# Strassen's seven block products for the feed-forward of a hybrid encoder block

## The chip, the core and the metric

One core of a Trainium2 chip runs the whole block as one program. TensorE (PE) multiplies matrices, VectorE (DVE), ScalarE (ACT) and GpSimd (POOL) do the element-wise work, SyncE (SP) issues the transfers between DRAM and the on-chip memory (SBUF) on one queue, which 16 DMA engines work off. Matrix products are accumulated in PSUM, eight banks of 128 x 512 float32. The metric is the device time in microseconds (us), as the median of several executions. One execution is profiled; its rows stand below.

## The reference, cut to what matters

For one sequence of 2048 tokens with 1024 features, all in float32:

```python
mod = silu(c) @ w_ada + b_ada                      # shift, scale, gate for two sub-layers
x = x + gate1 * (mixer(rms_norm(x) ...) @ w_out)   # recurrent and attention heads
h2 = rms_norm(x, norm2_g) * (1.0 + scale2) + shift2
ff = jnp.square(jax.nn.relu(h2 @ w_ff1)) @ w_ff2   # 1024 -> 4096 -> 1024
x = x + gate2 * ff
return rms_norm(x, final_g)
```

The change touches the last four lines.

## The kernel before, in words

A product of two float32 matrices is made from three products of rounded halves: each operand is split into a high part (a copy in the rounded type `F32R`) and a low part (the operand less its high part, rounded in turn), and PE adds high x high, high x low and low x high in one PSUM bank. So a block of 128 x 128 x 512 costs three matmuls of 512 columns. Every matmul is issued by the helper `mm` (line 87); the splits of weights are made by `wsplit` (line 240): the high part by ACT (line 91), the low part in two pieces of 512 columns by POOL (line 250) or in one by DVE (line 252).

The program is traced in Python. Its tiles are named by a tag (`sbt`), each tag has a fixed number of buffers (`BUFS`), and a planner sets the order of the instructions on each engine from the order in which they are traced, from its own costs and from when buffers come free. An engine, and SP's queue as well, then works off its instructions in that fixed order; one that waits holds those behind it. `later`, `tick`, `side` and `step` spread small pieces of work between larger ones while the program is traced.

In the mixer's output stage `out_a` makes one tile of 128 tokens after another (24 matmuls each; tiles 8 to 15 first, then 0 to 7). `norm2` normalises it. Tiles 8 to 15 are stored in DRAM (`Dx1`); tiles 0 to 7 stay in SBUF, in the four accumulators `acc_`. `build` transposes four tiles at a time by PE (line 315, four transposes to a bank) and splits the result (lines 332 to 334) into `h2T`.

The feed-forward runs over two halves of 1024 tokens, first tiles 0 to 7, then 8 to 15. In each half it goes through the 32 groups of 128 hidden columns. `ff1` multiplies a group's weights, from DRAM, with the half's tokens, in two groups of 512 tokens with 24 matmuls each, then squares the positive part (ACT lines 1257 and 1258, DVE line 1259, POOL line 1260 for the low part). `ff2_tile` multiplies the group's hidden block with the second layer's weights, which `ff_w2` has scaled by the gate (line 245): per tile of tokens two banks of 3 matmuls (6 for the first and last two groups), each added by DVE to its accumulator (line 1276), which starts as the residual. So nothing of the hidden layer leaves SBUF. The second layer of one group runs between pieces of the first layer of the next. When a half is through, `final` normalises each tile (POOL line 294, DVE lines 292 to 299 and 1291) and stores it (line 1292).

Of the kernel before, what the change touches and what calls it, by code (L numbers as in the profile page):

```python
# [56 lines left out]
def block_kernel(ctx: ExitStack, tc, x, vecs, pos, w_ada, b_ada, fg, w_in, lwa, lwx, w_out, w1, w2, cst, out):  # L57
# [3 lines left out]
    sb = ctx.enter_context(tc.tile_pool(name="sb", bufs=1))  # L61
# [7 lines left out]
    def sbt(tag, shape, dt=F32):  # L69
        cnt[0] += 1  # L70
        return sb.tile(list(shape), dt, tag=tag, name=f"{tag}_{cnt[0]}", bufs=BUFS[tag])
# [62 lines left out]
    Dx1 = [drt(f"Dx1{t}", (P, D)) for t in range(NT // 2)]  # L134
# [1026 lines left out]
    acc_ = [sbt("L8", (P, 2, D)) for _ in range(4)]  # L1161
    r2s = cpt("r2s", (P, 8))
    order = list(range(8, 16)) + list(range(8))
    la_ = {}

    def load_a(t):
        if t < 8:
            xt = acc_[t // 2][:, t % 2]
        else:
            if t % 2 == 0:  # L1170
                la_["pair"] = sbt("L8", (P, 2, D))
            xt = la_["pair"][:, t % 2]
# [4 lines left out]
    h2T = [None, None]  # L1177
    xn = {}

    def norm2(t, xt):  # L1180
# [3 lines left out]
        if t >= 8:  # L1184
            later(lambda: SY.dma_start(Dx1[t - 8], xt), 1)
        for r2 in rstd_g(ss, D, r2s[:, t - 8:t - 7] if t >= 8 else None):
            yield
        if t < 8:
            if t % 2 == 0:
                xn["pair"] = sbt("L8", (P, 2, D))  # L1190
            xn[t] = xn["pair"][:, t % 2]
            V.tensor_scalar(xn[t], xt, r2[:, 0:1], None, ALU.mult)
# [14 lines left out]
    bld = iter(())  # L1207
    for i, t in enumerate(order):
# [7 lines left out]
        out_a(t)  # L1216
        step(2)
        run(bld, 4)
        if i + 3 < NT:
            load_a(order[i + 3])  # L1220
        if t == 5:
            h2T[0] = new_hT()
            bld = build([xn[e] for e in range(4)], h2T[0], gs2, sh2)
    flush()
    run(bld)
    built = [last[:], None]
    h2T[1] = new_hT()
    bld = build([xn[e] for e in range(4, 8)], h2T[1], gs2, sh2)


    gate2 = sbt("bc", (P, D))
    SY.dma_start(gate2, Dbc[1])
    fgb = sbt("bc", (P, D))
    bcast_row(fgb, fg, D)

    def ff_w1(i):
        w = wsplit(wraw(w1[i]), A, G)
        return w.rearrange("p s (k c) -> p s k c", k=8)

    def ff_w2(i):  # L1240
        e = V if i < FV else G
        return wsplit(wraw(w2[i * P:(i + 1) * P, :]), A, e, row=gate2, row_eng=e)

    def ff1(w, hid, g):
        pt = pst("tr")
        n = 0
        hT = h2T[g]
        for k in range(8):
            hi, lo = hT[k // 4][:, k % 4, :], hT[2 + k // 4][:, k % 4, :]
            for l, r in ((w[:, 0, k, :], hi), (w[:, 0, k, :], lo), (w[:, 1, k, :], hi)):  # L1250
                mm(pt, l, r, n == 0, n == 23)
                n += 1
            if k % 4 == 3:
                if k == 7:
                    cs = slice(512 * g, 512 * (g + 1))
                    r_ = sbt("t2", (P, 512))
                    A.activation(r_, pt, AF.Relu)  # L1257
                    A.activation(hid[:, 0, cs], r_, AF.Square)
                    V.tensor_tensor(r_, r_, r_, ALU.mult)  # L1259
                    G.tensor_tensor(hid[:, 1, cs], r_, f(hid[:, 0, cs]), ALU.subtract)  # L1260
                yield

    nb = [0]

    def ff2_tile(t, parts):
        ts = slice(t * P, (t + 1) * P)
        for hf in range(2):
            cs = slice(512 * hf, 512 * (hf + 1))
            pt = pst("mm" if nb[0] % 2 else "g")
            nb[0] += 1  # L1270
            for i, (w, hid) in enumerate(parts):
# [6 lines left out]
    def ff2(parts):  # L1278
        for t in range(8):
            ff2_tile(t, parts)  # L1280
            if t % 2 == 1:
                yield
# [130 lines left out]
```

## Time and profile before

| | us |
|---|---|
| median of 3 runs | 2800.24 |
| lowest and highest | 2793.2, 2805.78 |
| the profiled execution | 2808.67 |
| its span, first to last instruction | 2806.9 |
| PE busy in it | 2685.0 |

In a page of the profile the busy time of an engine is its share of the span; the strips cut the span into 40 slices of 70 us and give tenths. A line such as L87 is that of the helper that issued the instruction, so groups are told apart by their tiles: `ptr<-hT,wh` are the first layer's matmuls, `pg<-wh,L` and `pmm<-wh,L` the second's. The mean of one matmul is longer than its place in the sequence, since they are pipelined; the place is had from a count over a stretch. In the rows of stretches come start and end, the length, for each engine the busy us and the number of instructions, then the granted clock (1.00 is 2.4 GHz), the share of the 16 DMA engines' time and GB/s.

### The profile page before, as it was taken

How to read it: one execution, taken by the hardware profiler on the slowest of the kernel's cores; microseconds unless marked ns; L12 is line 12 of the kernel's file. 1: busy time of each engine (PE TensorE's matmuls, PEld its weight loads, DVE VectorE, ACT ScalarE, POOL GpSimd, SP SyncE). 2: the span in 40 equal slices, each digit the busy share in tenths (PEclk: the TensorE clock that was granted, in tenths of full speed). 3: DMA queues.
4: the chain of work that ended last, by engine and by line, in shares of the span. 5: the costliest groups of instructions: out<-in, count | busy, mean ns of one | idle time of the engine just before them, and what ended most of it. 6: DMA issues, size and time to landing. Idle time of an engine off the chain costs nothing.

```text
span 2806.9 us, 33193 instructions
## 1 busy us (share of the span) xinstructions
PE 2685.0 (96%) x12089; PEld 2209.7 (79%) x12089; DVE 1645.0 (59%) x3174; ACT 801.2 (29%) x1173; POOL 1093.1 (39%) x833
## 2 busy tenths in 40 slices
PE   4988998999999999999899999999999999999998
PEld 3766777778888888878688888888878888888886
DVE  6688787965434444546645555555575555555555
ACT  2244675561222222223321112121142211211112
POOL 2443444632211221322444444444445444454442
PEclk9998999998899889899999999999999999999999
DMA  6765347566445545467111111111133111111111
GB/s 258 270 213 184 96 165 253 174 161 165 111 114 136 120 118 125 120 190 240 68 53 46 46 45 46 53 53 46 46 119 144 53 46 46 46 53 53 46 38 60
DMA packets 178783, 309.83 MB, mean 110 GB/s; under 512 B 79018, under 2 KB 112550, under 8 KB 171050
## 3 DMA queue, kind: packets, MB, share of 16 engines
q1 hardware_dynamic: 178620, 307.72, 35.2%
q8 instruction: 95, 1.56, 0.2%
q14 instruction: 68, 0.56, 0.1%
HBM read 230.83 MB, written 76.64 MB: 110 GB/s over the span
## 4 chain that ended last, share of the span: by engine, by line
PE 48%; DVE 2%; POOL 0%; issue 0%; ACT 0%; DMA 0%; POOLq 0%; DVEq 0%; ACTq 0%
PE ptr L87 24%; PE pg L87 12%; PE pmm L87 12%; DVE L L1276 0%; DVE L L1291 0%; POOL ry L294 0%; POOL hT L334 0%; DVE r L1300 0%; DMA r<-Dx 0%; POOL wh L250 0%; PE ptr L315 0%; DVE hT L334 0%; DVE hT L333 0%; ACT st L332 0%; DVE ry L299 0%
## 5 line engine op out<-in xcount | busy, mean ns | idle before, releaser
L250 POOL TENSOR_TENSOR wh<-r,wh 128x512 fp32r<-128x512 f32 x332 | 477.9, 1462 | 716.5 <-ACT wh L91 539.0
L87 PE MATMUL ptr<-hT,wh 128*128 128x512 f32 x3072 | 744.5, 392 | 4.0 <-POOL hT L334 2.1
L87 PEld LDWEIGHTS ptr<-hT,wh 128*128 128x128 f32 x3072 | 579.1, 189 | 129.2 <-ACT st L332 3.2
L1276 DVE TENSOR_TENSOR L<-pg,L 128x512 f32<-128x512 f32 x480 | 331.3, 690 | 565.3 <-PE pg L87 564.5
L87 PE MATMUL pg<-wh,L 128*128 128x512 f32 x1536 | 434.4, 394 | 0.0
L87 PE MATMUL pmm<-wh,L 128*128 128x512 f32 x1536 | 434.3, 394 | 0.0
L87 PE MATMUL pmm<-hT,wh 128*128 128x512 f32 x1536 | 377.6, 402 | 6.4 <-POOL hT L334 3.6
L1257 ACT ACTIVATE t<-ptr 128x512 f32<-128x512 f32 x128 | 76.8, 600 | 1003.4 <-PE ptr L87 1003.4
L87 PEld LDWEIGHTS pmm<-hT,wh 128*128 128x128 f32 x1536 | 294.8, 194 | 79.6 <-POOL hT L334 8.1
L87 PEld LDWEIGHTS pmm<-wh,L 128*128 128x128 f32 x1536 | 288.1, 188 | 68.8
L87 PEld LDWEIGHTS pg<-wh,L 128*128 128x128 f32 x1536 | 288.2, 188 | 66.6 <-POOL L L1260 0.4
L1276 DVE TENSOR_TENSOR L<-pmm,L 128x512 f32<-128x512 f32 x480 | 330.0, 688 | 10.5 <-PE pmm L87 8.6
L846 DVE CUSTOM_DVE_ANT_0 junk<-ptr,mb 128x256 bf16<-128x256 f32 (+2 forms) x384 | 140.1, 365 | 173.8 <-PE ptr L87 156.3
L1260 POOL TENSOR_TENSOR L<-t,L 128x512 fp32r<-128x512 f32 x128 | 166.9, 1305 | 179.0 <-DVE t L1259 179.0
L900 ACT ACTIVATE t<-pmm 128x512 f32<-128x512 f32 x160 | 95.1, 596 | 357.0 <-PE pmm L87 355.8
L294 POOL TENSOR_TENSOR ry<-rv,mhalf 128x1 f32<-128x1 f32 x80 | 52.3, 655 | 329.5 <-DVE rv L292 324.2
L87 PE MATMUL pmm<-hT,hT 66*128 66x256 f32 (+5 forms) x672 | 175.7, 396 | 0.0
L87 PE MATMUL ptr<-hT,hT 128*128 128x256 f32 (+5 forms) x672 | 163.2, 390 | 4.1 <-DVE mc L846 4.0
L87 PE MATMUL pg<-t,L 128*66 128x192 f32 (+2 forms) x756 | 156.6, 344 | 2.7 <-POOL L L1039 2.7
L91 ACT ACTIVATE wh<-r 128x1024 fp32r<-128x1024 f32 x128 | 135.1, 1057 | 80.7 <-PE pmm L87 69.2
L87 PEld LDWEIGHTS pmm<-hT,hT 128*128 128x128 f32 (+1 forms) x672 | 147.6, 276 | 8.4 <-issue 2.3
L87 PEld LDWEIGHTS ptr<-hT,hT 128*128 128x128 f32 (+1 forms) x672 | 142.0, 278 | 13.7 <-DVE mc L846 7.0
(211 smaller groups left out, 2990.3 us busy)
## 6 DMA issues: line engine op xcount, KB each, us to landing
r<-in_w SPq DMA_DIRECT2D x128, 512.0 KB
L<-in_w_ada SPq DMA_DIRECT2D x24, 1024.0 KB
r<-in_w_in SPq DMA_DIRECT2D x40, 512.0 KB
r<-in_x SPq DMA_DIRECT2D x26, 512.0 KB
hT<-Dq SPq DMA_DIRECT2D x21, 512.0 KB
hT<-Dk SPq DMA_DIRECT2D x21, 512.0 KB
Dh<-hT SPq DMA_DIRECT2D x8, 1024.0 KB
Dq<-st SPq DMA_DIRECT2D x32, 256.0 KB
```

The costliest lines, as they stand in the source:

```text
L87: T.matmul(o, l, r, start=st, stop=sp, skip_group_check=True)
L91: A.activation(o, i, AF.Copy)
L250: G.tensor_tensor(w[:, 1, cs], raw[:, cs], f(w[:, 0, cs]), ALU.subtract)
L294: G.tensor_tensor(y, v_, mhalf[:, 0:1], ALU.pow)
L846: V.tensor_tensor_reduce(junk[:, 0:nk], p_[:, e, 0:nk], mb1[:, off:off + nk], 1.0, -3e38, ALU.add, ALU.max, mc[:, idx:idx + 1])
L900: A.activation(pf, pS, AF.Exp)
L1257: A.activation(r_, pt, AF.Relu)
L1260: G.tensor_tensor(hid[:, 1, cs], r_, f(hid[:, 0, cs]), ALU.subtract)
L1276: V.tensor_tensor(o, pt, o, ALU.add)
```

## The change

Both layers are cut into 2 x 2 blocks and multiplied by Strassen's seven products. With A the weights or hidden blocks on the left and B the right operand, the tables `LEFT` and `RIGHT` name the one or two blocks that are added (or subtracted) for each product: (11, 1, 22) is block 11 plus block 22, (21, 0, 0) block 21 alone.

The mixer's output stage now keeps all 16 tiles' residual in DRAM (`Dx1`) and stores the normed and transposed tokens there too (`Dh2`, float32, unsplit). Then the buffers of the stages before are given up and laid out anew (`f1`). The first layer goes over two halves of 1024 tokens, in each over seven products, in each over 16 steps `p` of 128 hidden rows: a step adds its weight blocks, splits the sum, and issues 12 matmuls. The product's right operand is made once per product by `b_prep`, while the product before runs. `evac1` adds the bank to the blocks of the hidden layer that need it. Hidden blocks 12 and 21 are ready after products 3 and 4; they go to DRAM (`Dhh`) and are loaded again in products 6 and 7, where the seven left operands of the second layer are formed and stored (`Dhx`).

The second layer lays the buffers out once more (`f2`). It goes over seven products, each over 16 steps with 24 matmuls: eight tiles of tokens, each in its own PSUM bank, accumulate over the 16 steps. A step loads a hidden operand (512 KB) and one or two weight blocks. `evac2` adds the banks to the output tiles `C`. In the last product `finals` multiplies `C` by the gate, adds the residual and normalises; that product's own weights carry the gate.

```diff
-    Dx1 = [drt(f"Dx1{t}", (P, D)) for t in range(NT // 2)]
+    Dx1 = [drt(f"Dx1{t}", (P, D)) for t in range(NT)]
+    Dh2 = [{(k, j): drt(f"Dh2{a}{k}{j}", (P, 4, 512)) for k in (1, 2) for j in (1, 2)} for a in range(2)]
+    Dhh = [{i: drt(f"Dhh{a}{i}", (16, P, 512)) for i in (12, 21)} for a in range(2)]
+    Dhx = {m: drt(f"Dhx{m}", (16, P, 2, 512)) for m in range(1, 8)}
...
+    def build2(a, j, ts):
+        for k in range(8):
+            p_ = tr_bank(ts, k)
+            t = sbt("st", (P, 512))
+            A.activation(t, p_, AF.Identity, scale=gs2[:, k:k + 1], bias=sh2[:, k:k + 1])
+            yield
+            SY.dma_start(Dh2[a][k // 4 + 1, j][:, k % 4], t)
...
+        if i % 4 == 1 and i > 4:
+            t0 = order[i - 5]
+            bld.append(build2((i - 5) // 8, (i - 5) // 4 % 2 + 1, [xn[e] for e in range(t0, t0 + 4)]))
...
+    LEFT = {1: (11, 1, 22), 2: (21, 1, 22), 3: (11, 0, 0), 4: (22, 0, 0), 5: (11, 1, 12), 6: (21, -1, 11), 7: (12, -1, 22)}
+    RIGHT = {1: (11, 1, 22), 2: (11, 0, 0), 3: (12, -1, 22), 4: (21, -1, 11), 5: (22, 0, 0), 6: (11, 1, 12), 7: (21, 1, 22)}
+    stage.close()
+    NP = DFF // P // 2
+    BUFS.update({"c21": NP, "c11": NP, "c22": NP, "wr": 4, "wf": 3, "hx": 7})
...
+    def halves(raw, hi, lo, lo_eng):
+        A.activation(hi, raw, AF.Copy)
+        lo_eng.tensor_tensor(lo, raw, f(hi), ALU.subtract)
+    ORD1 = (2, 4, 5, 3, 1, 6, 7)
...
+    def w1_prep(s):
+        _, m, p = steps1[s]
+        x_, y_ = raws1.pop(s)
+        if LEFT[m][1]:
+            t = sbt("st", (P, 512))
+            signed(V, t, x_, LEFT[m][1], y_)
+        else:
+            t = x_
+        w = sbt("wf", (P, 2, 512), F32R)
+        halves(t, w[:, 0], w[:, 1], V if m == 7 else G)
...
+    def b_prep(a, m):
+        hi, lo = sbt("L8", (P, 4, 512), F32R), sbt("L8", (P, 4, 512), F32R)
...
+        for k in range(4):
+            t = sbt("st", (P, 512))
+            SY.dma_start(t, Dh2[a][x_ // 10, x_ % 10][:, k])
+            if sg:
+                t2 = sbt("st", (P, 512))
+                SY.dma_start(t2, Dh2[a][y_ // 10, y_ % 10][:, k])
+            yield
+            if sg:
+                signed(V, t, t, sg, t2)
+            halves(t, hi[:, k], lo[:, k], V)
+            yield
...
+    def evac1(s, pt):
...
+        elif m == 3:
+            h = c.pop((12, p))
+            V.tensor_tensor(h, pt, h, ALU.add)
+            V.tensor_tensor(c[22, p], pt, c[22, p], ALU.add)
+            yield
+            sq_relu_v(h)
+            yield
+            SY.dma_start(Dhh[a][12][p], h)
...
+        elif m == 6:
+            h = c[22, p]
+            V.tensor_tensor(h, pt, h, ALU.add)
+            sq_relu_a(h)
+            yield
+            x2, x7 = hx.pop((s, 12)), hx.pop((s, 21))
+            V.tensor_tensor(x2, x2, h, ALU.add)
+            V.tensor_tensor(x7, x7, h, ALU.subtract)
+            yield
+            put(a, 4, p, h)
+            put(a, 2, p, x2)
+            put(a, 7, p, x7)
+        else:
+            h, h22 = c.pop((11, p)), c.pop((22, p))
+            V.tensor_tensor(h, pt, h, ALU.add)
+            sq_relu_a(h)
+            yield
+            x1_, x5, x6 = sbt("st", (P, 512)), hx.pop((s, 21)), hx.pop((s, 12))
+            V.tensor_tensor(x5, x5, h, ALU.add)
+            G.tensor_tensor(x1_, h, h22, ALU.add)
+            G.tensor_tensor(x6, x6, h, ALU.subtract)
+            yield
+            put(a, 3, p, h)
+            put(a, 5, p, x5)
+            put(a, 1, p, x1_)
+            put(a, 6, p, x6)
...
+    LW, LP = 4, 2
...
+    for s, (a, m, p) in enumerate(steps1):
...
+        if s + LW < N1:
+            w1_load(s + LW)
+        if s + 2 < N1:
+            hx_load(s + 2)
+        if s + LP < N1:
+            w1_prep(s + LP)
...
+        for k in range(4):
+            ks = slice(k * P, (k + 1) * P)
+            for l, r in ((w[:, 0, ks], hi[:, k]), (w[:, 0, ks], lo[:, k]), (w[:, 1, ks], hi[:, k])):
+                mm(pt, l, r, n == 0, n == 11)
+                n += 1
...
+    BUFS.update({"C": NT, "xr": 4, "w2": 4, "wf": 4, "xt": 2, "row": 2})
+    ORD2 = (4, 2, 7, 3, 5, 1, 6)
...
+    def prep2(s):
...
+            signed(V, t, x_, RIGHT[m][1], y_)
+            if m == 6:
+                V.tensor_tensor(t, t, gate2[:, 512:], ALU.mult)
...
+        halves(t, w[:, 0], w[:, 1], V)
...
+        A.activation(h[:, 0], r_, AF.Copy)
+        for e in range(2):
+            G.tensor_tensor(h[:, 1, e], r_[:, e], f(h[:, 0, e]), ALU.subtract)
...
+    def resid(t, eng):
+        xt = sbt("xt", (P, D))
+        SY.dma_start(xt, Dx1[t])
+        yield
         for hf in range(2):
             cs = slice(512 * hf, 512 * (hf + 1))
+            eng.tensor_tensor(C[t][:, cs], C[t][:, cs], gate2[:, cs], ALU.mult)
+        yield
+        for hf in range(2):
+            cs = slice(512 * hf, 512 * (hf + 1))
+            eng.tensor_tensor(C[t][:, cs], C[t][:, cs], xt[:, cs], ALU.add)
...
+    for s, (m, p) in enumerate(steps2):
+        if s + L2 < N2:
+            ld2(s + L2)
+        if s + P2 < N2:
+            prep2(s + P2)
+        w, h = wts2.pop(s), hids.pop(s)
+        if p == 0:
+            pts = [pst(("mm", "g", "tr")[i % 3]) for i in range(8)]
+        for i in range(8):
+            ts = slice(i * P, (i + 1) * P)
+            mm(pts[i], h[:, 0, ts], w[:, 0], p == 0, False)
+            mm(pts[i], h[:, 0, ts], w[:, 1], False, False)
+            mm(pts[i], h[:, 1, ts], w[:, 0], False, p == NP - 1)
+            if p == NP - 1:
+                evac2(m, i, pts[i])
+                if m == 6:
+                    step(2)
+        if m == ORD2[-1]:
+            if p == 0:
+                fin = finals()
+            if p >= 1:
+                run(fin, 6)
```

Where the loads and stores of a step go: `w1_load` loads one or two blocks of 128 x 512 from `w1` (two of one row block in one transfer), `hx_load` the two blocks of `Dhh` in products 6 and 7, `put` stores a block in `Dhx`, `ld2` loads a hidden operand of `Dhx` and one or two blocks of `w2`.

## Rows read from the trace of the kernel before

**Rows 1.** The page: busy time of the engines; the granted clock in 40 slices.

```profile
PE 2685.0 (96%) x12089; PEld 2209.7 (79%) x12089; DVE 1645.0 (59%) x3174; ACT 801.2 (29%) x1173; POOL 1093.1 (39%) x833
PEclk9998999998899889899999999999999999999999
```

**Rows 2.** Busy time by stretch, the feed-forward in full run.

```profile
core 0: us, PE busy (x) PEld busy (x) DVE busy (x) ACT busy (x) POOL busy (x), PEclk, DMA share, GB/s
1500.00:1700.00 200.00, 200.00 (x869) 162.95 (x869) 108.34 (x162) 39.24 (x54) 93.80 (x63) 1.00 0.14 48
```

**Rows 3.** Groups by line, 1352-2807 us: count | busy us, mean ns | idle.

```profile
L87 PE MATMUL ptr<-hT,wh 128*128 128x512 f32 x3072 | 744.5, 392 | 4.0 <-POOL hT L334 2.1 <-ACT st L332 1.4 <-DVE hT L333 0.4
L87 PE MATMUL pg<-wh,L 128*128 128x512 f32 x1536 | 434.4, 394 | 0.0
L87 PE MATMUL pmm<-wh,L 128*128 128x512 f32 x1536 | 434.3, 394 | 0.0
L1276 DVE TENSOR_TENSOR L<-pg,L 128x512 f32<-128x512 f32 x480 | 331.3, 690 | 565.3 <-PE pg L87 564.5
L1259 DVE TENSOR_TENSOR t<-t 128x512 f32<-128x512 f32 x128 | 95.8, 749 | 42.1 <-ACT L L1258 42.1
L250 POOL TENSOR_TENSOR wh<-r,wh 128x512 fp32r<-128x512 f32 x240 | 333.6, 1413 | 538.5 <-ACT wh L91 538.5
L1257 ACT ACTIVATE t<-ptr 128x512 f32<-128x512 f32 x128 | 76.8, 600 | 1003.4 <-PE ptr L87 1003.4
L1291 DVE SCALAR_TENSOR_TENSOR L<-L,ry,bc 128x1024 f32<-128x1024 f32 x16 | 20.5, 1281 | 0.3
```

**Rows 4.** PE in order of time: start us, us, line, operation, tiles, count.

```profile
646.45 8.12 PE L87 MATMUL ptr<-L,L 128*128 128x256 f32 x36
...
1344.58 3.90 PE L87 MATMUL pmm<-hT,r 128*128 128x512 f32 x16
1349.79 0.66 PE L315 MATMUL ptr<-ck,L 128*128 128x128 f32 x4 [0.43 <-ACT st L332]
...
2794.57 1.55 PE L87 MATMUL pmm<-wh,L 128*128 128x512 f32 x6
```

**Rows 5.** Busy time by stretch, the feed-forward's start and its middle.

```profile
1360.00:1380.00 20.00, 16.72 (x81) 12.38 (x82) 15.98 (x18) 8.92 (x13) 14.07 (x7) 1.00 0.15 53
2080.00:2100.00 20.00, 15.51 (x60) 10.88 (x59) 16.01 (x32) 5.18 (x8) 8.07 (x6) 0.74 0.47 177
```

**Rows 6.** Busy time by stretch: full queues, storing of k, the mixer's output.

```profile
10.00:15.00 5.00, 0.00 (x0) 0.00 (x0) 4.76 (x12) 0.00 (x0) 0.00 (x0) 1.00 1.02 410
215.00:220.00 5.00, 5.00 (x8) 2.16 (x8) 2.17 (x4) 2.23 (x4) 0.00 (x0) 0.50 1.00 318
582.00:582.50 0.50, 0.50 (x3) 0.41 (x2) 0.37 (x1) 0.50 (x2) 0.00 (x0) 0.50 0.52 180
582.50:583.00 0.50, 0.50 (x3) 0.41 (x2) 0.00 (x0) 0.50 (x2) 0.00 (x0) 0.50 0.52 197
1285.00:1315.00 30.00, 29.15 (x133) 23.68 (x132) 19.66 (x76) 8.91 (x15) 5.82 (x11) 1.00 0.86 264
```

**Rows 7.** SP's queue in order of time: loads, a store of k.

```profile
161.34 2.19 SPq L346 DMA_DIRECT2D r<-in_x  x4
...
581.23 0.58 SPq L408 DMA_DIRECT2D Dk<-st  x1
```

**Rows 8.** POOL and DVE in order of time, side by side and apart.

```profile
1422.21 3.00 POOL L250 TENSOR_TENSOR wh<-r,wh 128x512 fp32r<-128x512 f32 x2
1422.69 1.37 DVE L1259 TENSOR_TENSOR t<-t 128x512 f32<-128x512 f32 x1 [5.49 <-ACT L L1258]
...
1607.16 0.69 DVE L1259 TENSOR_TENSOR t<-t 128x512 f32<-128x512 f32 x1
```

**Rows 9.** Busy time by stretch, TensorE idle, and at its low clock.

```profile
210.00:215.00 5.00, 0.48 (x1) 0.48 (x2) 4.47 (x11) 1.64 (x3) 0.00 (x0) 0.77 0.91 271
645.00:650.00 5.00, 5.00 (x24) 4.99 (x22) 3.92 (x17) 0.00 (x0) 0.00 (x0) 0.50 1.03 280
```

More of the change, by code (lines that the diff above doesn't have):

```diff
@@ L1175, in load_a @@
         la_[t] = [xt, st_, None, False]
-    h2T = [None, None]
-    xn = {}
     def norm2(t, xt):
@@ new lines, in block_kernel, with w1_load @@
+    steps1 = [(a, m, p) for a in range(2) for m in ORD1 for p in range(NP)]
+    raws1, wts1, bks = {}, {}, {}
+    def w1_load(s):
+        _, m, p = steps1[s]
+        x_, sg, y_ = LEFT[m]
+        t = sbt("wr", (P, 2, 512))
+        if sg and x_ // 10 == y_ // 10:
+            u = p + NP * (x_ // 10 - 1)
+            SY.dma_start(t.rearrange("p a c -> p (a c)"), w1[u])
+            raws1[s] = (t[:, x_ % 10 - 1], t[:, y_ % 10 - 1])
+            return
+        for i, blk in enumerate((x_, y_) if sg else (x_,)):
+            k = blk % 10 - 1
+            SY.dma_start(t[:, i], w1[p + NP * (blk // 10 - 1)][:, 512 * k:512 * (k + 1)])
+        raws1[s] = (t[:, 0], t[:, 1])
@@ new lines, in block_kernel @@
+    N1 = len(steps1)
+    LW, LP = 4, 2
+    for s in range(LW):
+        w1_load(s)
+    run(b_prep(0, ORD1[0]))
+    for s in range(LP):
+        w1_prep(s)
+    after, bp, prev = [], iter(()), None
+    for s, (a, m, p) in enumerate(steps1):
+        if p == 2:
+            nxt = steps1[s + NP - 2][:2] if s + NP - 2 < N1 else None
+            bp = b_prep(*nxt) if nxt is not None else iter(())
+        if s + LW < N1:
[4 more added lines that the diff above has]
+            w1_prep(s + LP)
+        w, (hi, lo) = wts1.pop(s), bks[a, m]
+        pt = bank()
+        n = 0
+        for k in range(4):
+            ks = slice(k * P, (k + 1) * P)
+            for l, r in ((w[:, 0, ks], hi[:, k]), (w[:, 0, ks], lo[:, k]), (w[:, 1, ks], hi[:, k])):
+                mm(pt, l, r, n == 0, n == 11)
+                n += 1
+        after = [g for g in after if run(g, 1)]
+        if prev is not None:
+            g = evac1(*prev)
+            if run(g, 1):
+                after.append(g)
+        prev = (s, pt)
+        run(bp, 1)
@@ new lines, in block_kernel @@
+    after.append(evac1(*prev))
+    while after:
+        after = [g for g in after if run(g, 1)]
+    st1.close()
+    BUFS.update({"C": NT, "xr": 4, "w2": 4, "wf": 4, "xt": 2, "row": 2})
+    sb[0] = ctx.enter_context(tc.tile_pool(name="f2", bufs=1, reuse_waits="tile"))
+    ORD2 = (4, 2, 7, 3, 5, 1, 6)
+    steps2 = [(m, p) for m in ORD2 for p in range(NP)]
+    N2 = len(steps2)
+    C = {}
+    gate2, fgb = sbt("row", (P, D)), sbt("row", (P, D))
+    raws2, wts2, hraw, hids = {}, {}, {}, {}
@@ L1285, in final @@
+    def final(t):
+        xt = C[t]
         cnt[0] += 1
@@ new lines, in final, with finals @@
+        SY.dma_start(out[t * P:(t + 1) * P, :], xt)
+    def finals():
+        for t in TILES[2]:
+            yield from resid(t, V)
+            yield
+        for t in TILES[1]:
+            yield from resid(t, V)
+            yield from final(t)
+    L2, P2 = 3, 2
+    for s in range(L2):
+        ld2(s)
+    SY.dma_start(gate2, Dbc[1])
+    bcast_row(fgb, fg, D)
+    for s in range(P2):
+        prep2(s)
+    fin = None
+    for s, (m, p) in enumerate(steps2):
[20 more added lines that the diff above has]
+                run(fin, 6)
@@ L1366, in block_kernel @@
+    run(fin)
     flush()
```

253 lines of the change are left out of this document (113 added, 140 removed).

## The prediction

> **What bounds the kernel now.** I read the page first: TensorE (PE) is busy 96% of the span, and from the middle of the span on its slices are full at the full granted clock [rows 1]. Those slices are the feed-forward, so the second view is the busy time by stretch: in 200 us of it PE is busy 200.00 us with 869 matmuls, while VectorE (DVE) has 108, GpSimd (POOL) 94 and ScalarE (ACT) 39 us of the 200 and the transfers take 0.14 of the queues' time [rows 2]. That is 200/869 = 0.230 us for a matmul of 512 columns, and nothing else is near its limit. The third view, the groups by line, counts them: 3072 + 1536 + 1536 = 6144 matmuls [rows 3], so 6144 x 0.230 = 1414 us are bound by nothing but PE. The mixer's last output matmul ends at 1344.58 + 3.90 = 1348.5, the feed-forward's last at 2794.57 + 1.55 = 2796.1 [rows 4]; of these 1447.6 us, 33 are not matmuls of the feed-forward: transposes and waits at its start and between its halves (81 PE operations, transposes among them, in 20 us and 60 in 20 us, where 87 are usual) [rows 5]. After the last matmul come 2806.9 - 2796.1 = 10.8 us of normalising and storing.
>
> **The change, part by part.** The sum is made against the profiled execution's 2808.7 us (span 2806.9); the median of the runs shown is 2800.2, that is 8.4 less, which I take off at the end.
>
> *Matmuls.* Seven block products in place of eight, in both layers: the first layer issues 2 halves x 7 x 16 steps x 12 = 2688 matmuls, the second 7 x 16 x 24 = 2688. 6144 - 5376 = 768 go: 768 x 0.230 = **-177 us**. A step of the first layer is 12 matmuls, 2.76 us; a block product's 16 steps are 44.2 us. A step of the second is 24 matmuls, 5.52 us, and 16 of them 88.4 us. All that follows asks what else fits into these.
>
> *Transfers of the first layer.* A step loads one or two weight blocks of 256 KB; in products 2, 4, 5, 3 and 1 the transfers come to 9 or 10 MB in 44.2 us (weights 4 or 8 MB, the next product's operand 1 or 2 MB, hidden blocks stored in two of the products 4 MB), up to 237 GB/s, which PE covers. Products 6 and 7 are another matter. A step of 6 loads 512 KB of weights, reloads two hidden blocks (512 KB) and stores three (768 KB); a step of 7 loads as much and stores four (1 MB). With the next operand (2 and 1 MB) that is 31.5 MB and 34.6 MB (10^6 bytes) in 44.2 us each: 712 and 783 GB/s. The trace never moves that much: with the queues full it shows 410 GB/s with rows of 4 KB, and 318 in a mixed stretch [rows 6]. For rows of 2 KB, which nearly all of these transfers have, the nearest row is the storing of the k columns in 2 KB pieces [rows 7]: 180 GB/s at 0.52 of the queues [rows 6], so 346 full; the stretch after it gives 197 at 0.52, together some 362. I take 365. Both halves need 131 MB here; 4 MB a half are loaded ahead under product 1 (seven reload buffers, four weight buffers), 2 MB drain under the next half's first product: 121 MB. At 365 GB/s they take 332 us, and PE has 4 x 44.2 = 177 us to cover them: **+155 us** of stalled PE. The ends are 410 GB/s (+118) and 318 (+204). SP's queue has 8.5 transfers a step to issue, 0.55 us each at the rate of four in 2.19 us [rows 7], 4.7 us, under the 5.4 and 5.8 us that the bytes take; the stores wait there for DVE with the next loads behind them, which is in the lower end's rate.
>
> *Engines in the first layer.* DVE's 512-wide operations are 0.69 us [rows 3]. In products 3 and 1 it has 2 to 4 of them a step, 2.76 us while the next operand is split: as much as PE. Beside a POOL subtraction an operation with two SBUF inputs took 1.37 us, and 0.69 alone [rows 8]. That would make some 3.4 us of eight steps each; eight PSUM banks let the results wait. I take **+5** (0 to 25). In 6 and 7 DVE needs 3.1 to 3.5 us a step, up to 4.5 beside POOL, and POOL in 7 two operations of 1.3: above PE's 2.76, below the transfers, so nothing is added, and if the transfers were free this would be the bound instead, at about +80 us.
>
> *Start.* The normed tiles of both halves are now transposed in the mixer's output stage and stored. The same 128 transposes: 24 of the 32 banks of four fall between the output tiles, 0.66 us each [rows 4], 16 us, the last 8 after them, 5 us; the first half's operand is ready long before, so a bubble of 5 us for the first weights (their buffers come free with the last output tile; 0 to 20, since that stage's transfers are at 264 GB/s and 0.86 already [rows 6] and get 12 MB more). Sum 26 where 33 stood: **-6** (-12 to +15).
>
> *Between the layers.* The second layer's first load waits behind the last stores, then one sum, one copy, two subtractions (0.69 + 0.6 + 2 x 1.3 us): **+8** (3 to 20).
>
> *Second layer.* 109 MB in 620 us, DVE 1.4 and POOL 2.6 us a step of 5.52: covered, except where a product ends. All eight banks are in use, and products 5 and 1 take each out with two DVE operations: 8 x 1.38 = 11 us where PE needs the first again after 5.5: **+5** (0 to 10).
>
> *The end.* In the last product's 88.4 us DVE gets the former product's banks (11 us), 14 weight tiles of three operations (29), gate and residual of 16 tiles, four operations each (44), eight final norms (1.28 us and five short ones of 0.16, 16.6), and after the last matmuls eight additions and eight more norms (22): 123 us, 34 more than PE, and 4 for the store. The 73 us of them with two SBUF inputs meet POOL in half of the time; the row's mean beside POOL is 749 ns where it could be 690 [rows 3], the worst case is double. With a fifth added the end comes 50 us after the last matmul, not 10.8: **+40** (+10 if the planner finds gaps, +70 at worst).
>
> *Sum.* -177 + 155 + 5 - 6 + 8 + 5 + 40 = +30: 2838.7 against 2808.7, **2830 us** as a median. (About 0.5%, 14 us, is what a measurement of this kernel can tell from no change.)
>
> One rule speaks against the change more strongly. The Trainium skill, DMA: Bandwidth & Descriptors, section Rules for kernel authors, asks for 1 MiB or more in one DMA, and its section Measured (for another way of issuing) gives 138 GB/s for 64 KB and 341 for 1 MB; between them I estimate 250 for 256 KB, by which the term of +155 would be 308 and the sum 2983. The trace disagrees for transfers that overlap: pieces of 256 KB ran at 180 GB/s on half of the queues.
>
> **The rivals.**
> A. *The transfers run at their best rate.* Products 6 and 7 keep the queues full at 410 GB/s: +118, and the median comes to 2793. For it: the loads of 4 KB rows ran so [rows 6]. Against it: rows of 2 KB, and loads and stores mixed. It decides at 400 GB/s; above, the kernel is not slower than before.
> B. *The clock.* PE works 2.8 us and waits 2.6 or more. After PE had been idle for most of 5 us the granted clock was at 0.50, the 1.2 GHz level [rows 6, 9], and over a stretch with 15.5 of 20 us busy its mean was 0.74 [rows 5]. At 0.50 [rows 9] 36 matmuls of 256 columns took 8.12 us [rows 4], so 12 of 512 take 5.4. If the clock stays there through 6 and 7, PE's step is as long as the transfers'; they overlap, yet each now waits for the other, and I take half of the 2.65 us lost: 64 x 1.3 = +85, 2915. The Trainium skill, TensorE: Matmul & The Clock Gate, section HAM oscillation, tells of such waits for DMA as a loop that keeps the clock low; that agrees with the row.
> C. *The end is covered.* The planner places gate and residual in DVE's gaps (DVE is 54% busy now [rows 2]), so that only additions and norms are left: +10 in place of +40, 2800: no change.
> D. *Stores and loads take turns.* A reload waits until an earlier store from its buffer has landed, at the head of SP's queue, and holds the weight loads behind it; the queues run empty meanwhile and the rate is 318 GB/s or less: +204 or more, 2879 at 318. For it: the stretch at 318 with a full share [rows 6]. Against it: the loads that need no reload buffer are four steps ahead. The Trainium skill's rule on small transfers, above, would come true in this way.
>
> **How the numbers follow.** Forecast 0.40, A 0.18, B 0.12, C 0.15, D 0.15. Faster needs A or C with luck, or both together (2763): 0.20. No change takes most of C, half of A and a little of the forecast: 0.20. Slower is the rest, 0.60. For eight times in ten I go from A and C together, 2765, to B, 2915. The forecast's own range is 2800 to 2865.
>
> **What would show it.** PE: 5376 matmuls of 512 columns, 0.230 us each outside of products 6 and 7. In the stretches of those four block products the queues' share near 1 at 340 to 390 GB/s, and each 80 to 95 us long; the other ten near 44. The waits: PE waiting for weights split by ACT and POOL, and these for transfers. At the end DVE busy without a gap, the last matmul some 50 us before the end. The forecast is wrong if products 6 and 7 stay under 75 us each (A), if PE's clock is 0.50 there and the queues are under 0.8 (B, or D with the clock up), or if the end takes under 25 us (C).

## The result, and the profile after

The changed kernel takes **2923.35 us** (median of 4, 2920.59 to 2927.24), the kernel before 2799.57: 1.0443 times as long, 95% interval 1.0416 to 1.0471. 2830 was predicted, with 2765 to 2915. The direction is right, the size is not: 118.5 us lie between the two profiled executions (2927.2 and 2808.7) where the sum had 30.

The page of the changed kernel, its strips in 40 slices of 73 us, answers to [rows 1]. PE is no longer full from the middle on: twice its slices fall to 4 to 8 tenths, with the clock, and there the transfers are mostly at 8 or 9 tenths. The bytes have doubled to 599 MB (310 before).

```profile
PE 2624.2 (90%) x11321; PEld 2110.6 (72%) x11321; DVE 1701.3 (58%) x3074; ACT 1017.0 (35%) x1573; POOL 1107.1 (38%) x867
PE   4988899999999999998999766999864999999996
PEclk9999999988998888998999967999966999999998
DMA  6764537554555554687568899668888846535554
DMA packets 329703, 599.32 MB, mean 205 GB/s; under 512 B 95786, under 2 KB 129318, under 8 KB 321962
```

The busy time by stretch, cut at the first matmul of a block product, answers to [rows 2, 5, 6] (columns as there). First an undisturbed product 4, then products 6 and 7 of the first half and product 2 of the second, then 6 and 7 of the second half; after them 20 us between the layers, the second layer's third product, and its last.

```profile
1421.50:1465.90 44.40, 44.40 (x193) 36.00 (x193) 24.20 (x32) 18.35 (x33) 21.56 (x16) 1.00 0.63 206
1612.30:1682.00 69.70, 52.87 (x193) 37.65 (x191) 47.33 (x64) 30.22 (x51) 19.60 (x14) 0.93 0.85 277
1682.00:1795.20 113.20, 74.47 (x192) 50.99 (x192) 58.90 (x72) 31.77 (x52) 35.40 (x25) 0.73 0.91 295
1795.20:1866.10 70.90, 58.44 (x192) 43.20 (x193) 26.66 (x31) 29.57 (x55) 34.72 (x25) 0.81 0.82 282
2058.60:2128.10 69.50, 53.84 (x193) 38.28 (x191) 49.85 (x65) 30.25 (x51) 19.24 (x14) 0.90 0.87 282
2128.10:2246.50 118.40, 78.37 (x192) 52.94 (x192) 42.88 (x65) 27.24 (x45) 35.51 (x28) 0.71 0.82 279
2252.00:2272.00 20.00, 0.00 (x0) 0.00 (x0) 2.77 (x4) 1.54 (x2) 1.85 (x2) 0.50 1.01 344
2452.90:2542.20 89.30, 89.30 (x385) 72.17 (x384) 40.32 (x51) 26.50 (x35) 46.60 (x32) 1.00 0.55 189
2810.20:2907.60 97.40, 92.21 (x385) 72.88 (x383) 89.37 (x149) 31.12 (x47) 53.63 (x33) 0.98 0.51 183
```

Products 6 and 7 take 70 and 113 to 118 us, 370.8 together, where PE alone needs 4 x 44.4 = 177.5. No engine is busy for all of that time, and the queues' share is 0.82 to 0.91 at 277 to 295 GB/s.

PE in order of time answers to [rows 4]: the mixer's last output matmuls, the first of the feed-forward, two steps of the second product 7, the start of the second layer, and the last matmuls.

```profile
1346.76 5.25 PE L89 MATMUL pmm<-hT,r 128*128 128x512 f32 x22
...
1371.95 6.10 PE L89 MATMUL pg<-L,wf 128*128 128x512 f32 x12 [8.62 <-ACT wf L1258]
...
2234.47 4.78 PE L89 MATMUL pg<-L,wf 128*128 128x512 f32 x12 [2.71 <-ACT wf L1258]
2241.95 4.55 PE L89 MATMUL pmm<-L,wf 128*128 128x512 f32 x12 [2.71 <-ACT wf L1258]
...
2272.09 2.15 PE L89 MATMUL pmm<-wf,L 128*128 128x512 f32 x3 [25.58 <-ACT L L1464]
...
2906.71 0.86 PE L89 MATMUL pg<-wf,L 128*128 128x512 f32 x3
```

From these times each term of the sum is measured. A matmul's place is 0.2311 us here (44.4 / 192), so 5376 are 1242 us against 1414.

| term | predicted | measured | how |
|---|---|---|---|
| matmuls | -177 | -172 | 1242 - 1414 |
| transfers of products 6 and 7, with the drain | +155 (118 to 204) | +220 | 370.8 - 177.5, and 70.9 - 44.4 for product 2 after them |
| start | -6 | -7 | 3.5 (mixer ends later) + 20.0 + 3.3 (first step at the clock of 0.50) - 33.6 |
| other products | +5 (0 to 25) | +30 | nine of them 432.8 - 399.6, less the 3.3 above |
| between the layers | +8 (3 to 20) | +26 | 2272.1 - 2246.5 |
| second layer | +5 (0 to 10) | +14 | 635.5 - 621.2 |
| end | +40 (10 to 70) | +7 | 17.9 - 10.8 |

They sum to +118. So four terms were too small by 117 us and one too large by 33; the transfers alone miss by 65.

What the waits look like there: SP's queue in the first product 7, then in the second (longest first: us in total, times, longest).

```profile
SPq L1328 <- DMA Dhx<-hx: 35.1, 29, 3.1
```

```profile
SPq L1331 <- DVE hx L1379: 33.8, 10, 5.1
SPq L1328 <- DMA Dhx<-hx: 18.5, 30, 2.4
```

In the first, SP issues 127 transfers in 68 us, 0.53 us each (the 73.6 in e6's expectation counts more than the issuing), and waits for 40: it has no free moment in 113 us. That alone shows no limit: in the undisturbed product 4 it issues for 10 us, 0.35 us a transfer, and waits for 31 of the 44, mostly to load weights into a buffer that is still in use. What differs is the wait: 35 of the 40 us are waits of a reload until the store out of its buffer has landed, at the head of the queue. In the second, a store stands at the head and waits for VectorE's sum.

And what VectorE does there, in order of time in the second product 7: a step of 7.5 us in which it waits for the matmuls, empties the bank (L1375), adds a reloaded block (L1379), and only then sums the next step's weights (L1254). ScalarE's copy follows (the 0.76 us), and PE starts when that is through: 12 matmuls of about 4.7 us, at a clock that has fallen (0.71 on the mean of this product), alternate with 2.7 us of preparation. The planner put the weights behind the evacuation; the two steps of lead in the traced program are gone.

```profile
2231.80 0.69 DVE L1375 TENSOR_TENSOR c<-pmm,c 128x512 f32<-128x512 f32 x1 [4.23 <-PE pmm L89]
2232.41 0.68 DVE L1379 TENSOR_TENSOR hx<-hx,c 128x512 f32<-128x512 f32 x1
2233.01 0.68 DVE L1254 TENSOR_TENSOR st<-wr 128x512 f32<-128x512 f32 x1
2234.45 0.69 DVE L1259 TENSOR_TENSOR wf<-st,wf 128x512 fp32r<-128x512 f32 x1 [0.76 <-ACT wf L1258]
2239.28 0.69 DVE L1375 TENSOR_TENSOR c<-pg,c 128x512 f32<-128x512 f32 x1 [4.14 <-PE pg L89]
```

So three causes stand beside each other: the rate of the bytes (R), one issuing queue on which loads and stores wait for each other (the prediction's D), and the loop of matmuls and weights, with the low clock (L, and the prediction's B).

### The profile page after: what moved, and what is told of

Read it like the earlier page. It is cut to its first block, busy times and chain, and to the rows that moved or that the text cites. A ratio compares the mean times of both kernels' runs of the same rounds, so it can differ in the third digit from the quotient of the medians.

```text
span 2925.5 us, 33421 instructions
## 1 busy us (share of the span) xinstructions
PE 2624.2 (90%) x11321; PEld 2110.6 (72%) x11321; DVE 1701.3 (58%) x3074; ACT 1017.0 (35%) x1573; POOL 1107.1 (38%) x867
## 4 chain that ended last, share of the span: by engine, by line
PE 25%; DMA 8%; DVE 7%; issue 7%; POOL 6%; ACT 2%; SPq 1%; POOLq 0%; DVEq 0%; ACTq 0%
PE pmm L89 11%; PE pg L89 9%; PE ptr L89 5%; POOL wf L1259 5%; DMA Dhx<-hx 3%; DMA st<-Dh 2%; DVE st L1254 2%; DMA hx<-Dhh 1%; DMA wr<-in_w 1%; ACT wf L1258 1%; POOL L L1466 1%; DMA r<-Dat 1%; SPq L1331 1%; POOL ry L301 0%; DVE hx L1368 0%
## 5 line engine op out<-in xcount | busy, mean ns | idle before, releaser
L1466 POOL TENSOR_TENSOR L<-xr,L 128x512 fp32r<-128x512 f32 x224 | 328.1, 1486 | 291.7 <-ACT L L1464 285.8
L89 PE MATMUL pg<-L,wf 128*128 128x512 f32 x1008 | 284.0, 431 | 58.9 <-ACT wf L1258 47.7
L89 PE MATMUL pmm<-L,wf 128*128 128x512 f32 x1008 | 285.4, 434 | 56.4 <-ACT wf L1258 46.1
L89 PE MATMUL pmm<-wf,L 128*128 128x512 f32 x1008 | 291.7, 397 | 30.9 <-ACT L L1464 25.6
L89 PEld LDWEIGHTS pg<-L,wf 128*128 128x128 f32 x1008 | 205.1, 208 | 128.2 <-ACT wf L1258 59.0
L89 PEld LDWEIGHTS pmm<-L,wf 128*128 128x128 f32 x1008 | 206.9, 209 | 124.3 <-ACT wf L1258 57.2
L89 PE MATMUL pg<-wf,L 128*128 128x512 f32 x1008 | 289.9, 396 | 0.0
L89 PEld LDWEIGHTS pg<-wf,L 128*128 128x128 f32 x1008 | 190.1, 189 | 45.3
L257 POOL TENSOR_TENSOR wh<-r,wh 128x512 fp32r<-128x512 f32 x88 | 140.7, 1621 | 176.7 <-DVE wh L95 105.2
L89 PE MATMUL ptr<-wf,L 128*128 128x512 f32 x672 | 193.6, 396 | 0.0
L1254 DVE TENSOR_TENSOR st<-wr 128x512 f32<-128x512 f32 x160 | 158.4, 1006 | 57.1 <-DMA wr<-in_w 28.0
```

The costliest lines, as they stand in the source:

```text
L89: T.matmul(o, l, r, start=st, stop=sp, skip_group_check=True)
L257: G.tensor_tensor(w[:, 1, cs], raw[:, cs], f(w[:, 0, cs]), ALU.subtract)
L1254: eng.tensor_tensor(o, a, b, ALU.add if sign > 0 else ALU.subtract)
L1466: G.tensor_tensor(h[:, 1, e], r_[:, e], f(h[:, 0, e]), ALU.subtract)
```

## The experiments

Every run's time, and from PE's timeline the length of its products 6 and 7 (first matmul to the next product's first), of product 2 of the second half, and the gap between the layers. One execution each, but for the changed kernel and e13, of which the time is the median of four and the lengths are from the profiled one; a single execution can differ by some 0.3%, 8 us. The expectations of e1, e2 and e4 take 362 us for the four products; counted as here they are 371.

| run | time | 6, 7, 6, 7 | sum | product 2 | gap |
|---|---|---|---|---|---|
| changed kernel | 2923 | 69.7, 113.2, 69.6, 118.4 | 371 | 70.9 | 25.6 |
| e1 weights first | 2904 | 66.2, 110.9, 67.5, 104.6 | 349 | 70.3 | 28.8 |
| e2 narrow stores | 2847 | 61.2, 87.4, 60.6, 99.2 | 308 | 63.0 | 17.1 |
| e3 both of these | 2826 | 55.9, 84.7, 56.7, 81.3 | 279 | 67.3 | 16.9 |
| e4 half the matmuls | 2904 | 70.6, 109.7, 69.0, 97.4 | 347 | 69.3 | 30.3 |
| e5 more reload buffers | 2948 | 72.4, 120.1, 69.2, 135.5 | 397 | 71.2 | 13.4 |
| e6 second queue | 2874 | 73.3, 95.0, 74.8, 82.7 | 326 | 64.6 | 22.4 |
| e7 four blocks | 2746 | 49.5, 48.1, 47.9, 45.5 | 191 | 47.0 | 9.6 |
| e8 four blocks, early residual | 2747 | 48.7, 49.0, 49.5, 44.5 | 192 | 46.2 | 9.5 |
| e9 narrow, second queue | 2797 | 57.7, 75.3, 57.7, 75.3 | 266 | 55.8 | 14.5 |
| e10 weights first, second queue | 2868 | 72.4, 92.2, 73.4, 82.1 | 320 | 66.0 | 23.6 |
| e11 four blocks, deeper buffers | 2692 | 45.0, 47.9, 45.6, 44.5 | 183 | 45.8 | 9.5 |
| e12 as e10, half the matmuls | 2867 | 73.1, 94.8, 73.2, 82.4 | 324 | 66.7 | 24.5 |
| e13 as e11, four executions | 2696 | 45.5, 48.0, 44.5, 44.5 | 183 | 45.8 | 10.3 |

**e1, the weights first.** Edges in the instruction order, with nothing waited for, put the weight sum and copy of step s+3 ahead of the evacuation of step s:

```diff
+            e_ = V.tensor_tensor(h, pt, h, ALU.add)
+            r_, _ = sq_relu_a(h)
+            if s + 3 in preps:
+                behind(e_, preps[s + 3][0])
+                behind(r_, preps[s + 3][1])
```

> One change to the changed kernel: on VectorE and ScalarE the weight sum and the high copy of step s+3 are ordered ahead of the addition that empties the bank of step s (and its relu), in block products 6 and 7; the bytes stay as they are. In the changed kernel these two products take 66.6 and 115 us in the first half, 67.4 and 113.5 in the second (362.5 together, 177 would be TensorE alone). Theory R (the transfers' rate): the queues move some 300 to 325 GB/s whatever the order, so the four stay within 15 us of 362 and the time within 2905 to 2925. Theory L (order): in product 7 the next step's weights are made only after the step before has been evacuated, so that 12 matmuls (5 us at the low clock) and some 3 us of preparation alternate; without that a step is 12 matmuls at the full clock or the transfers at 365 GB/s, 95 us a product 7 at most: the time falls by 40 us or more, to 2880 or less.

Measured: 2903.8, the four products 349 us. That is R's side, though 22 us go, 14 of them in the second product 7, where the loop was. The order is a small part of the loss.

**e2, narrow stores.**

```diff
-        SY.dma_start(Dhx[m][p][:, a], t)
+        SY.dma_start(Dhx[m][p][:, a, 0:32], t[:, 0:32])
...
-        SY.dma_start(hraw[s], Dhx[m][p])
+        SY.dma_start(hraw[s].rearrange("p a c -> p (a c)"), w1[p + NP * (m % 2)])
```

> The stores of the seven left operands of the second layer are cut to 32 of 512 columns, and the second layer reads as many bytes of the first layer's weights in their place (so its products are of other numbers); the order of the work on VectorE is that of the changed kernel. Product 6 then moves 18.9 MB in place of 31.5, product 7 17.8 in place of 34.6. Theory R: at 300 to 325 GB/s these take 58 to 63 and 55 to 59 us, the four 226 to 244 in place of 362, and the time is about 2795 (less still if the gap between the layers, which no longer waits for stores, closes by up to 18 us). Theory L: the loop of matmuls, evacuation and weight preparation is as long as before, product 7 stays at 105 us or more, and the time at 2890 or more.

Measured: 2846.5, the four 308 us. Neither theory: with 40% to 49% of the bytes gone product 7 still takes 87 and 99 us, where 55 to 59 were expected of the rate. The queues' share is 0.57 to 0.76 there, so they are not full, and the number of transfers is as before.

**e3, both.**

> Both edits together: weights ordered ahead of the evacuation, and the stores of the left operands cut to 32 of 512 columns (the second layer reads the first layer's weights in their place). Theory R: as with the narrow stores alone, within 15 us. Theory L: clearly less than with either alone, products 6 and 7 at 50 to 60 us each, the time at 2770 or less. If both matter, this is the only one of the three near TensorE's 44 us a product.

Measured: 2825.5, 279 us: less than with either, but product 7 is still at 81 to 85 us. So neither bytes nor the order of the weights is all of it. In the first product 7 SP issues 127 transfers in 50 us and waits 28 of the 84.7.

**e4, half the matmuls** (`if m < 6 or n in (0, 2, 4, 7, 9, 11):` ahead of `mm`).

> Products 6 and 7 issue 6 of their 12 matmuls a step (so part of the sum is left out); transfers and the rest are unchanged. Theory R: the transfers set the pace, the four stretches stay within 15 us of 362, the time at 2905 to 2925. Theory L: a step of product 7 loses the 2.5 us or more of the matmuls left out, 16 x 2.5 = 40 us in each half, and the time falls to 2845 or less.

Measured: 2904.4, 347 us. PE is busy 27 us less in each product 7. The first hardly changes for it (109.7), the second loses 21 us. So PE's time, and the low clock with it, counts in the second product 7 and nowhere else.

**e5, more reload buffers.**

```diff
-                hx[s, i] = sbt("hx", (P, 512))
+                hx[s, i] = sbt("hx" if i == 21 else "c21", (P, 512))
...
-        if s + 2 < N1:
-            hx_load(s + 2)
+        if s + 4 < N1:
+            hx_load(s + 4)
```

> The same bytes and the same transfers as the changed kernel; only the reloaded blocks get 23 buffers in place of 7 (half of them in the buffers of c21, free in these products) and are loaded four steps ahead in place of two. Theory D (stores and loads take turns): SyncE waits at the head of its queue for stores out of the reload buffers to land, 35 us in the first product 7 and 97 in the stage; these waits go, and products 6 and 7, 371 us together in the changed kernel, fall by 50 us or more: 2870 or less. Theory R (rate of the bytes, some 325 GB/s when the queues are full): the queues have a share of 0.9 already, so at most 25 us go: 2900 or more.

Measured: 2947.8, 397 us, slower than without: above R's bound, though R has no reason for a loss. The edit did not do what it was made for: of the reloads' waits for a store to land, 28.5 us of 35.1 are left in the first product 7 and 13.8 of 18.5 in the second. So it can't tell what these waits cost. In the second product 7 the head of the queue is then blocked by something else, stores that wait for GpSimd's sum and weights that wait for VectorE's (SP's waits there):

```profile
SPq L1331 <- POOL st L1380: 32.4, 10, 7.3
SPq L1277 <- DVE st L1254: 22.7, 8, 3.8
SPq L1328 <- DMA Dhx<-hx: 13.8, 9, 2.0
```

**e6, a second queue.** The same bytes and buffers; one name changes (the planner's order around it follows):

```diff
     def put(a, m, p, t):
-        SY.dma_start(Dhx[m][p][:, a], t)
+        A.dma_start(Dhx[m][p][:, a], t)
```

> The same bytes; the stores of the left operands (3 a step in product 6, 4 in product 7) are issued by ScalarE's queue in place of SyncE's. Theory S (one issuing queue is full): in the first product 7 SyncE issues 129 transfers in 73.6 us and waits for 38, 112 of 113 us; with 64 or so fewer transfers on it, products 6 and 7 fall by 50 us or more, to 2870 or less. Theory R: the bytes are the same, at most 25 us go: 2900 or more. ScalarE waiting for VectorE and GpSimd before a store may hold its copies of the weights back, which would make it slower than the changed kernel, 2930 to 2960.

Measured: 2874.0, the four products 45 us less, product 2 after them 6 less: a little short of theory S's 50, and far from R. The stretches (6, 7, 6, 7), and the longest of SP's waits in the first product 7:

```profile
1614.60:1688.00 73.40, 55.01 (x194) 38.22 (x192) 49.06 (x69) 24.98 (x45) 19.98 (x14) 0.91 0.94 326
1688.00:1783.00 95.00, 61.46 (x193) 40.60 (x193) 59.78 (x68) 28.91 (x53) 34.01 (x24) 0.86 0.97 332
2038.80:2113.60 74.80, 56.10 (x194) 39.42 (x192) 47.91 (x69) 24.96 (x45) 19.06 (x14) 0.89 0.93 321
2113.60:2196.30 82.70, 59.11 (x192) 39.35 (x192) 59.67 (x62) 27.12 (x48) 37.49 (x26) 0.90 0.99 347
```

```profile
SPq L1328 <- DMA Dhx<-hx: 61.5, 30, 5.3
```

The queues' share is now 0.93 to 0.99 where it was 0.82 to 0.91. The rate over the share, an estimate of what full queues move, changed less: 324 to 340 GB/s in the four stretches with one queue, 342 to 351 with two. (The 344 between the layers, in the row at 2252, is of stores first and of loads then.) SP's own queue still stands at the reloads' waits, longer than before; but the stores go on beside it, and the DMA engines stay busy. So the second queue fills the time in which the one stood. That is D, in a wider form than predicted: not the reload's wait alone, but all that holds up the only queue. A wait at its head is one such thing, slower issuing another: in the first product 7 a transfer took 0.53 us to issue on the one queue, 0.37 on each of the two. The run does not separate these.

The Trainium skill, DMA: Bandwidth & Descriptors, section Rules for kernel authors, says that spreading DMAs over issuing engines doesn't help the bandwidth and saves issue time only. On the rate of full queues the runs agree within some 5%. The 51 us that go do not contradict it either, since SP issues for 20 us in the first product 7 where it did for 68; how much of the 51 is issue time and how much is waiting stays open.

**e9, narrow stores on the second queue.**

> The narrow stores (32 of 512 columns; the second layer reads the first layer's weights in place of the left operands) and the stores on ScalarE's queue together. Products 6 and 7 take 371 us in the changed kernel, 308 with narrow stores alone, 326 with the second queue alone. If the bytes (at some 340 GB/s with full queues) and the turns on the single issuing queue are two limits, each of which holds when the other is taken away, the four fall to 200 to 250 us together, and the time to 2750 or less. If both edits only lighten one limit, they stay at 280 or more, and the time above 2790.

Measured: 2796.8, 266 us, between the two. The narrow stores alone had taken off 62, the queue alone 45; together 105. So they add up, as two separate losses would. What is left is probably VectorE's: it is busy 61.56 of 75.2 us in the first product 7, and of the 20 us that PE waits there 14 end with VectorE's split of the weights. No run takes that work away alone.

```profile
1667.80:1743.00 75.20, 55.52 (x192) 39.57 (x192) 61.56 (x71) 29.98 (x53) 34.84 (x24) 0.89 0.82 253
```

**e10 and e12, the rate alone.** The second queue with the weights first (e10), and that with half the matmuls (e12).

> All bytes; the stores on ScalarE's queue, and the weights of step s+3 ordered ahead of the evacuation of step s. If with two issuing queues only the rate of the bytes is left (share of the queues 0.93 to 0.99 at 321 to 347 GB/s), the order changes nothing more: products 6 and 7 at 310 to 330 us, the time 2860 to 2880. If the order (and with it the clock) still costs, the four fall below 300 and the time below 2850.

> All bytes, stores on ScalarE's queue, weights ahead of the evacuation (the kernel with 320 us for products 6 and 7), and in these products only 6 of the 12 matmuls of a step, so part of the sum is left out. If the rate of the bytes alone sets these 320 us, they stay at 305 to 330. If TensorE's time (at a clock that fell, 0.86 to 0.90 there) still has a share, 64 steps lose up to 1.4 us each: 290 or less.

Measured: 320 and 324 us. Both are as the first theory had it. With two queues the order brings 6 us at most, and half of the matmuls nothing, at a share of 0.93 to 0.98 in both. PE's busy time falls by a fifth to a quarter only, since the clock falls with its work: e12's four stretches have a mean granted clock of 0.55 to 0.61, near the 1.2 GHz level, and are hardly longer for it (3 us in all). Products 6 and 7 of the first half, in e10 and then in e12:

```profile
1609.50:1681.90 72.40, 54.97 (x193) 38.72 (x191) 47.68 (x68) 24.92 (x45) 19.10 (x14) 0.91 0.94 329
1681.90:1774.20 92.30, 61.13 (x193) 42.93 (x194) 61.78 (x66) 29.75 (x53) 36.95 (x25) 0.80 0.97 338
1606.80:1680.00 73.20, 41.26 (x98) 24.49 (x96) 49.76 (x69) 24.51 (x45) 20.09 (x14) 0.61 0.93 322
1680.00:1774.80 94.80, 48.86 (x96) 27.68 (x96) 63.07 (x66) 29.06 (x53) 36.03 (x24) 0.55 0.95 332
```

e10's four stretches move 107 MB at a share of 0.96, and no engine is full in them. So 320 us is about what these bytes cost, at some 345 GB/s over the share: 320.2 - 177.5 = 143, and 22 in product 2, some **165 of the 220**. The other 55 are what the second queue (51, e6) and then the order of the weights (4, e10) took off: the single queue's turns and, in the second product 7, the loop.

**e7, four stored blocks.** Here the first layer stores each hidden block once; the second layer loads one or two and adds them:

```diff
+    Dhb = {i: drt(f"Dhb{i}", (16, P, 2, 512)) for i in (11, 12, 21, 22)}
+    HID = {1: (11, 1, 22), 2: (12, 1, 22), 3: (11, 0, 0), 4: (22, 0, 0), 5: (11, 1, 21), 6: (12, -1, 11), 7: (21, -1, 22)}
...
+        for i in (x_, y_) if sg else (x_,):
+            hraw[s].append(sbt("xr", (P, 2, 512)))
+            SY.dma_start(hraw[s][-1], Dhb[i][p])
...
+        if HID[m][1]:
+            signed(V, r_[0], r_[0], HID[m][1], r_[1])
```

> The first layer stores each hidden block once (four blocks in place of seven sums and two blocks that are reloaded); the second layer loads one or two blocks a step and adds them on VectorE (80 sums of 1024 columns). Products 6 and 7 then move 14.7 and 13.6 MB in place of 31.5 and 34.6, and SyncE issues 3.3 transfers a step in place of 8. Every theory that blames the transfers of products 6 and 7, by rate or by queue, gives 44 to 50 us for each of the four (371 us become 176 to 200) and no slow start of the second half (26 us): 2700 to 2750, if the sums add up to 21 us at the end, where VectorE was full. If the order of the weights alone kept product 7 slow, it stays at 70 us or more there and the time is above 2780.

Measured: 2746.2, against 2795.9 for the kernel before beside it, 1.8% less, and within the forecast. Bytes, transfers and sums of products 6 and 7 all went together here, so this run does not tell them apart. The four products fall to 191 us, product 2 to 47.0, the gap between the layers to 9.6. The second layer pays: 669 us for 635, since VectorE waits for the hidden blocks (142 us in 53 waits) with the evacuation of banks behind them in its order.

**e8, the residual early** (half of `resid`'s work in products 3 and 1).

> As the four blocks, and half of the gating and residual additions (32 operations of 512 columns) are moved from the last product into products 3 and 1 of the second layer. If VectorE's work in the last product sets the end, this is 15 to 25 us faster than the four blocks alone; if the matmuls set it, the same within 5 us.

Measured: 2746.6, the same. The last product, in which VectorE is busy 99 of 106 us with the four blocks, gets 5.3 us shorter; the two products before it take 3.6 us more. So the work was moved, and the 15 to 25 us were not there to be had.

**e11 and e13, deeper buffers.** With 6 raw and 4 split weight buffers, loads 5 and splits 3 steps ahead, and 8 hidden buffers in the second layer:

```diff
-    LW, LP = 4, 2
+    LW, LP = 5, 3
...
-    L2, P2 = 3, 2
+    L2, P2 = 4, 2
```

> The four stored blocks with the early residual, and the space of the reload buffers given to others: first layer six raw and four split weight buffers, loads five and splits three steps ahead; second layer eight hidden buffers and loads four steps ahead. The four blocks had 28 us of gaps in the second layer, where VectorE waited 142 us for hidden blocks with the evacuation of banks queued behind these waits, and 58 us beyond the matmuls in the first. If the late loads cause these, the gaps halve and the time is 2700 to 2730; if VectorE's own work at the ends of the products does, it stays within 8 us of 2746.

> The four stored blocks with deeper buffers again, timed against the kernel before: one execution took 2692.5 us. Expected 2685 to 2700, 0.960 to 0.966 of the kernel before.

Measured: 2692.5, and timed 2696.46 (2695.86 to 2702.4) against 2798.64: **0.9642**, 95% interval 0.9625 to 0.9659. That is below what e11's forecast had (2700 to 2730). The ten products other than 6 and 7 went from 486 us (e8) to 455, with 444 for the matmuls; the second layer from 667 to 656. Products 6 and 7 of the first half in e13:

```profile
1597.50:1643.00 45.50, 45.24 (x194) 35.73 (x193) 29.84 (x45) 27.84 (x47) 17.70 (x13) 1.00 0.84 279
1643.00:1691.00 48.00, 45.72 (x193) 35.59 (x192) 32.12 (x51) 32.75 (x55) 3.87 (x3) 1.00 0.92 320
```

PE is nearly full, at 2.4 GHz, beside transfers of 279 to 320 GB/s.

## Why the prediction was wrong

- *Matmuls, start*: right, -172 and -7 for -177 and -6.
- *Transfers of the first layer*: the step that failed, +155 for +220. It named the right place and the right bytes, and its rate is near what full queues give (365 taken; over the share 324 to 340 measured with one queue, some 345 with two); with two queues and the weights first (e10) the term is some 165, near the 155. Wrong was that the kernel would keep the queues full. The prediction counted SP's time to issue, 4.7 us a step, found it under the bytes' 5.8, and let the one hide the other; the waits of stores and reloads at the head of the queue it put at nothing in the sum ("which is in the lower end's rate"). On the one queue, worked off in order, a wait and the next transfers' issuing come after each other: in the first product 7 SP issues for 4.2 us a step and waits for 2.5, and the step takes 7.1 (7.4 in the second). With the stores on a second queue it takes 5.9 and 5.2 (e6), near the bytes' 5.8.
- *Rival D* (2879 or more, 0.15) holds the measured term, +204 or more, and e6 shows what it is about: the one queue leaves the DMA engines without work at times. Its detail, the reload that waits for its buffer, is there in the rows (35.1 us), but no run shows what it costs by itself: e5 left most of these waits in place.
- *Rival A* is out: 277 to 295 GB/s, and 347 at the best. *Rival B*'s 2915 is nearest to the measured 2923, but by luck: e12 halves the matmuls and gains nothing, so PE's time does not set the pace. It counts in the second product 7 alone, up to 21 us (e4), not 85. The Trainium skill's HAM oscillation (TensorE: Matmul & The Clock Gate), cited for B, agrees with the fallen clock in the rows; but in e12 the low clock costs nothing, and in e13, where the transfers leave PE hardly any wait, the clock is at 1.00 in the same products.
- The signs that were to tell the rivals apart did not: product 6 stayed under 75 us (70), as for A, product 7 far above it, and the queues' share of 0.82 to 0.91 lay between the forecast's (near 1) and that of B and D (under 0.8). The 80 to 95 us a product hold for the mean of the four, 93, and for none of them.
- *VectorE as the next bound*: the prediction said that with free transfers it would cost +80. e9 comes nearest to that case: 266 - 177.5 = +89, with VectorE at 61.6 of 75 us; but the queues' share is still 0.73 to 0.82 there, so this is not shown.
- *Other products*, +30 for +5: the excess was looked for in products 3 and 1, for their evacuations. Product 3 has none (44.0 and 44.4 us); the excess lies in products 5 and 1 (49.5 to 54.1 us) and a little in the first product 2, which all add two weight blocks a step. It is weights that come a little late, not VectorE's contention in itself: operations did stretch as in [rows 8], the weight sums' mean is 1006 ns where 690 is usual, but in e11 it is still 944, and with more lead these products take 30 us less than in e8.
- *Between the layers*, +26 for +8: the step counted one load, sum and copy, and left out the backlog. The last stores are issued until 2263.9, 17 us after the last matmul; only then comes the first load of the second layer. Without that backlog (e7) the gap is 9.6.
- *The end*, +7 for +40, and *second layer*, +14 for +5, belong together: 8.6 of the 14 us lie in the last product (97.4 where its matmuls need 88.7), in which VectorE is busy 89.4 us and PE waits 5 us, mostly for weights that VectorE has yet to split. 2.7 lie in the first product, 0.6 to 0.7 in each of the others. So with VectorE's work the end cost some 15 us more than the 10.8 of before, not 40. Rival C held in its time and half in its mechanism: the planner drew 16 of the 32 gating operations ahead of the last product's first matmul, but only 2 of the 32 additions of the residual; 8 of the 16 final norms came after the last matmul, as the prediction had it.

The end's term, 33 us too large, made up for half of the 65 that the transfers missed: 2830 came from errors of both signs.

## What to carry to other kernels

A rate read where the queues are full is a ceiling; a term made from it needs the share at which the kernel will keep them, and a single in-order queue that carries loads and stores which wait for compute does not keep them full (0.82 to 0.91 here, 0.93 to 0.99 with the stores on a second one). Before sizing a burst of transfers, ask whether the sums have to be stored at all: four blocks stored once and added by the reader moved the work to the other layer, which took 34 us more for it, and together with deeper buffers made a change that cost 4.4% gain 3.6% (1.8% without the deeper buffers). A planner may order an engine's work otherwise than it was traced, so a lead in the traced program has to be looked for in the trace.

## What the runs showed of the hardware

- Mixed loads and stores of 256 KB, nearly all in rows of 2 KB, ran at 347 GB/s with the queues' share at 0.99 (e6, two issuing queues). Over the share that is 342 to 351 in e6's four stretches; with one queue, at shares of 0.82 to 0.91, 324 to 340.
- A store's size hardly matters to the queue that issues it: in e3's first product 7 a store of 32 columns took SP 0.38 to 0.41 us, a full load 0.35 to 0.42. The load on the queue does: 0.35 us a transfer in the changed kernel's undisturbed product 4, 0.53 in its first product 7 with all transfers on one queue (share 0.91), 0.37 on each of two queues in e6 (share 0.97).
- TensorE at a mean clock of 0.55 to 0.61 (e12) lost 3 us at most over products 6 and 7, since transfers set the pace; the clock alone, read in a page, would have pointed to the wrong cause.
